# A hybrid decoder layer in float32: linear attention's state formed once per 128 tokens instead of twice, with ten warm-up matmuls, more buffers for the memory's weights, and norms begun three steps later

## The chip, the core and the metric

The kernel runs on one core of one Trainium2 chip. The metric is the device time of one execution in microseconds (us), as the median of several runs. The core's engines are called by short names: PE is TensorE's matmuls, PEld its weight loads, DVE is VectorE, ACT is ScalarE, POOL is GpSimd and SP is SyncE, which here only issues transfers (DMAs).

## What is computed

One decoder layer over 256 tokens of width 2048, in float32. The change touches branch A, the gated linear attention (4 heads, keys of 128, values of 256). With `b` the running sum of the log decay inside a chunk, the reference works on chunks of 64 tokens:

```python
q_e = qc * jnp.exp(b);  k_e = kc * jnp.exp(-b);  k_d = kc * jnp.exp(b_last - b)
s = jnp.where(causal, einsum('bhncd,bhnsd->bhncs', q_e, k_e), 0.0)
o_intra = einsum('bhncs,bhnsv->bhncv', s, vc)
def step(S, inp):                       # once per chunk
    o = einsum('bhcd,bhdv->bhcv', qe, S)
    S = S * dec[..., :, None] + einsum('bhcd,bhcv->bhdv', kd, vv)
    return S, o
```

Branch B is stick-breaking attention (8 heads of 128, queries and keys normed per head). Branch C is softmax attention into 256 memory tokens (4 heads of 256, queries and keys normed), whose keys and values are `rmsnorm(mem) @ w_mem_kv`. Each branch is projected back to 2048, the three are merged by sigmoid gates, projected by `w_o` and added to x; a SwiGLU block of width 5632 follows. Nearly all of the arithmetic is in these dense products.

## The kernel before

**Dense products.** A weight matrix lies in memory in blocks of 512 columns. One load (`raw`, 1 MB) brings 4 row chunks of 128 by 512. ACT makes a high part `wh` (L148) and DVE the rest `wl` (L149), two chunks at a time, and PE multiplies three times for each 128 tokens: high by high, weights' rest by high, high by rest. So one such split of two chunks feeds 12 matmuls of 512 columns in `gemm` (L221 to L223); in `sgemm`, which does one level of Strassen's scheme on 1024 columns, it feeds 6 or 12 (L262 to L265). In `sgemm`, `put` (L302 to L304) copies a finished product out of or into an accumulator. These 512-column matmuls are called the big matmuls below.

**Buffers.** `loads()` (L172) hands out `raw` tiles from the list `free_raw`: three in `ring1` from the start, more when later pools are opened by `widen`. The splits go into the `w` buffers of the same pools (four in `ring1`). PSUM has four `acc` and four `tmp` banks. `loads`, `parts` and every pool's tile wait for the former user of a buffer; SP issues loads in the order of the program.

**Order.** Everything that is not a big matmul is written as Python generators in a list `background`. `step()` advances the first of them by one `yield`, once after each split in `gemm` and `sgemm` (twice for `fine`), so that small work is woven in between big matmuls; `flush()` runs all that is left. What is written thus is then ordered on each engine by the framework's scheduler, which may bring an instruction forward on its own engine.

**Stages that the change touches**, in order of time: eight matmuls of zeros (L563, L564) while the first data comes; the memory's keys and values (`mk`, `mv`; `w_kv`, L584 to L610) with x being loaded beside them (`load_x`); the memory's queries `mq` (L718 to L720); then `sq`, `sk` and `sv_` by `wide` (`sgemm`), each with the work on the one before it in the background: `normed_T` (L489) squares a projection on ACT (L496), sums and scales it on DVE (L497 to L508) and turns it by PE transposes (L520, helper L441), and the memory's attention runs as `m_scores`, `m_turn`, `m_out`, head after head (L667 to L708). `m_out` copies its result to an `out` tile, of which there are two, and sends it off by a DMA from ACT (`put_out`, L640). In `sgemm`, `p6` (L335) has POOL add one weight tile to another by a DMA of 1 MB (L339). Further on, `gla()` (L818) runs beside the projections of branches C and B (`gemm` L974 and L991): for each of two blocks of 128 tokens (`t`), it makes the decay sums by matmuls with constant triangles (L837, L838, L842), the three scaled q and k, turns two of them (L858), forms the scores (L866), and then in two chunks of 64 tokens (`c`): output from the scores (L881), output from the state (L883), the state's increment (L888), and the state itself on DVE (L890, L893).

Of the kernel before, what the change touches and what calls it, by code (L numbers as in the profile page):

```python
# [59 lines left out]
def constants():  # L60
    i, j = np.arange(P)[:, None], np.arange(P)[None, :]
    same = (i // GC) == (j // GC)
    blocks = [
        i == j,
        i < j,
        (i <= j) & same,
        i > j,
        np.ones((P, P), bool),
        (i <= j) & same,
        (i > j) & same,  # L70
        (i // GC) == np.arange(P // GC)[None, :],
    ]
    scale = [1, 1, 1, 1, 1, 1 / TAU, 1 / TAU, 1 / TAU]
    return np.concatenate([b.astype(np.float32) * np.float32(s) for b, s in zip(blocks, scale)], 1)
# [3 lines left out]
def trunk(ctx: ExitStack, tc: tile.TileContext, a, out):  # L78
# [18 lines left out]
    def narrow(pool):  # L97

        for x in (free_raw, splits):
            x[:] = [y for y in x if y[0] is not pool]  # L100
        pool.release()

    pad = tc.alloc_tile_pool(name="pad", bufs=1, side="right")
# [12 lines left out]
    def tmp():  # L116
        return ps.tile([P, NB], F32, tag="tmp", name="tmp", bufs=4)
# [11 lines left out]
    def flush():  # L129
        while background:  # L130
            step()
# [39 lines left out]

    def loads():  # L172

        slot = pool, bufs = free_raw.pop(0)
        return pool.tile([P, KG, NB], F32, tag="raw", name="raw", bufs=bufs), lambda: free_raw.append(slot)

    def parts():

# [307 lines left out]
        for n in range(0, MIX, NB):  # L486
            evac(dst[:, :, n : n + NB], gemm(xs, w, c0 + n), rstd)

    def normed_T(dst, src, heads, dim, gain, scratch):  # L489


        ss = small.tile([P, 2, heads], F32, name="hn_ss")
        for t in range(2):
            for n in range(0, MIX, NB):
                sq = scratch()
                act.activation(sq[:], src[:, t, n : n + NB], AF.Square)  # L496
                dve.tensor_reduce(  # L497
                    ss[:, t, n // dim : (n + NB) // dim],
                    sq[:].rearrange("p (h d) -> p h d", d=dim),
                    axis=AX.X,  # L500
                    op=ALU.add,
                )
            yield
        y = rsqrt_mean(ss[:].rearrange("p t h -> p (t h)"), dim, 2 * heads)
        for t in range(2):
            v = src[:, t].rearrange("p (h d) -> p h d", h=heads)
            dve.tensor_tensor(
                v, v, y[:, t * heads : (t + 1) * heads].unsqueeze(2).to_broadcast([P, heads, dim]), op=ALU.mult  # L508
            )
            yield  # L510
        yield
        e = dim // P
        for c in range(0, 8, 2 * e):
            for q in range(e):

                p = tmp()
                for i in range(2):
                    ch = c + q + i * e
                    for t in range(2):
                        transpose(p[:, i * T + t * P : i * T + (t + 1) * P], src[:, t, ch * P : (ch + 1) * P])  # L520
                d = dst[:, c + q : c + q + e + 1 : e, :]
                act.activation(d, p[:].rearrange("p (c t) -> p c t", c=2), AF.Copy, scale=gain[:, q : q + 1])
                yield
# [20 lines left out]
    def section(name, tag):  # L544
        return sec.tile([P, 2, MIX], F32, tag=tag, name=name)
# [77 lines left out]
    def ra():  # L623
        return ring("ra", 4)

    def rb():
        return ring("rb", 2)
# [97 lines left out]
    wide(sq, O_SQ)  # L725
    flush()
    skT_sv = main.tile([P, 2, 2, MIX], F32, tag="resid", name="skT_sv")
    skT, sv_ = chunks(skT_sv[:, 0]), skT_sv[:, 1]
    sqT = chunks(section("sqT", "b")[:])
    sk = section("sk", "d")  # L730
    background.append(normed_T(sqT, sq, SH, SD, g_sqs, ra))
    wide(sk, O_SK)
# [77 lines left out]
    def pause(n):  # L810
        for _ in range(n):
            yield
# [5 lines left out]
    def gla():  # L818
        for t in range(2):
# [12 lines left out]
            lh, ll = rc(), rd()  # L832
            split(lh[:], ll[:], ls[:])
            yield from pause(4)
            b, bl, dc = tmp(), tmp(), tmp()
            for dst, w in ((b, tri), (bl, rest)):
                pe.matmul(dst[:], w, lh[:], start=True, stop=False)  # L837
                pe.matmul(dst[:], w, ll[:], start=False, stop=True)  # L838
            for h in range(GH):
                for i, l in enumerate((lh, ll)):  # L840
                    pe.matmul(
                        dc[:, 2 * h : 2 * h + 2], l[:, h * GDK : (h + 1) * GDK], ind, start=i == 0, stop=i == 1  # L842
                    )
            qe, ke, kd = ra(), ra(), ra()
            act.activation(qe[:], b[:], AF.Exp)
            act.activation(ke[:], b[:], AF.Exp, scale=-1.0)
            act.activation(kd[:], bl[:], AF.Exp)
# [4 lines left out]
            dve.tensor_tensor(kd[:], gqk[:, t, 512:], kd[:], op=ALU.mult)  # L852
            yield from pause(3)
            turned = []
            for src in (qe, ke):
# [3 lines left out]
                turned.append(rb()[:].rearrange("p (h t) -> p h t", h=GH))  # L859
                dve.tensor_copy(turned[-1].rearrange("p h t -> p (h t)"), p[:])  # L860
                yield from pause(2)
            qeT, keT = turned
            yield from pause(2)
            p = tmp()
            for h in range(GH):
                pe.matmul(p[:, h * P : (h + 1) * P], keT[:, h], qeT[:, h], start=True, stop=True)  # L866
            sT = ra()[:].rearrange("p (h t) -> p h t", h=GH)
            nc.gpsimd.memset(sT, 0.0)
            dve.copy_predicated(sT, causal4, p[:].rearrange("p (h t) -> p h t", h=GH))
# [3 lines left out]
            o = [tmp(), tmp()]  # L873
            ov = [o[h // 2][:, h % 2 * GDV : (h % 2 + 1) * GDV] for h in range(GH)]
            vh = [gv[:, t, h * GDV : (h + 1) * GDV] for h in range(GH)]
            for c in range(2):
                s = slice(c * GC, (c + 1) * GC)
                for h in range(GH):
                    if c == 0:

                        pe.matmul(ov[h], sT[:, h], vh[h], start=h % 2 == 0, stop=False, skip_group_check=True)  # L881
                    if (t, c) != (0, 0):
                        pe.matmul(ov[h][s], qeT[:, h, s], S[h][:], start=False, stop=c == 1, skip_group_check=True)  # L883
                if (t, c) != (1, 1):
                    d = [tmp(), tmp()]
                    for h in range(GH):
                        dh = d[h // 2][:, h % 2 * GDV : (h % 2 + 1) * GDV]
                        pe.matmul(dh, kd[s, h * GDK : (h + 1) * GDK], vh[h][s], start=True, stop=True)  # L888
                        if (t, c) == (0, 0):
                            dve.tensor_copy(S[h][:], dh)  # L890
                        else:
                            f = dec[:, 2 * h + c : 2 * h + c + 1]
                            dve.scalar_tensor_tensor(S[h][:], S[h][:], f, dh, op0=ALU.mult, op1=ALU.add)  # L893
                    yield from pause(3)
# [289 lines left out]
```

## Time and profile before

| What | Value |
| --- | --- |
| Median of 3 runs (lowest to highest) | 1633.13 us (1632.35 to 1633.36) |
| The profiled execution, its own time | 1632.16 us |
| Its span, first to last instruction | 1630.4 us |
| ACT busy | 1028.4 us (63%) |
| DMA share, first to last slice of 40 | 8 tenths in the first, between 4 and 8 after it, 2 in the last |
| From 0.24 to 5.4 us | start, zeros matmuls, first loads |
| From 5.4 to 103 us | memory's keys and values |
| From 157 to 292 us | `sq`, `sk`, `sv_` (most of them) |
| From 439 to 534 us | `gla()` beside the projections of branches C and B |

How to read the views quoted below: a row of the timeline is start, duration, engine, line, operation, output<-inputs, shape, count, and in brackets the engine's idle time before it and what ended that. A matmul's printed duration is from start to result; matmuls overlap, so what one costs in a stream is the distance from its start to the next start. One matmul of float32 operands that are not yet split is two records. The waits view gives the engine, its line, whom it waited for, the total in us, how often, and the longest. The chain view follows the work that ended last: start, length, what.

### The profile page before, as it was taken

Reading aid. Unit: us, or ns where it says so; the run is one execution under the profiler, and the core shown is the slowest. Engines: PE = TensorE matmul, PEld = TensorE weight load, DVE = VectorE, ACT = ScalarE, POOL = GpSimd, SP = SyncE. Lnnn points to the kernel's source line nnn. Section 1 sums busy time; section 2 is a strip of 40 time slices with the busy share of each in tenths; the row PEclk is TensorE's granted clock in tenths of the full one; section 3 lists DMA queues with packets and bytes.
Section 4 is the critical chain, followed back from the end, with each engine's and each line's share of the span. In section 5 each row is a group of like instructions: output and inputs, shape, how many; then the busy total and the mean of one; then the engine's idle time right before and its main releaser. Section 6 shows DMA issues by size and latency. Waiting matters only on the chain.

```text
span 1630.4 us, 19473 instructions
## 1 busy us (share of the span) xinstructions
PE 1620.5 (99%) x7266; PEld 1325.9 (81%) x7266; DVE 1331.5 (82%) x1526; ACT 1028.4 (63%) x1251; POOL 71.2 (4%) x93
## 2 busy tenths in 40 slices
PE   9999999999999999999999999999999999999999
PEld 6888778888877788888888888888888888888887
DVE  6867788877755788897897798988888989888994
ACT  7765576766744666666565566666666666666662
POOL 0000000000000000000000000000110000110000
PEclk9999999999999999999999999999999999999999
DMA  8795667656654888888657768687897687897682
GB/s 328 281 326 161 216 223 247 201 178 203 210 166 165 283 263 257 265 281 301 185 215 234 257 225 265 207 278 245 255 281 243 208 268 255 264 263 246 203 331 92
DMA packets 65888, 390.33 MB, mean 239 GB/s; under 512 B 7265, under 2 KB 13921, under 8 KB 21633
## 3 DMA queue, kind: packets, MB, share of 16 engines
q1 hardware_dynamic: 51344, 324.36, 53.0%
q0 software_dynamic: 11504, 61.87, 19.7%
q10 hardware_dynamic: 2944, 2.85, 0.5%
q8 instruction: 57, 0.93, 0.2%
q14 instruction: 39, 0.31, 0.1%
HBM read 325.09 MB, written 12.58 MB: 207 GB/s over the span
## 4 chain that ended last, share of the span: by engine, by line
PE 96%; DMA 1%; ACT 1%; DVE 1%; issue 0%; ACTq 0%; DVEq 0%
PE acc L262 19%; PE acc L265 19%; PE acc L264 19%; PE acc L221 6%; PE acc L222 6%; PE acc L223 6%; PE tmp L262 6%; PE tmp L265 6%; PE tmp L264 6%; PE tmp L441 2%; ACT wh L148 1%; DMA raw<-in_w_mem_kv 0%; DMA od_mem<-out 0%; DVE wl L149 0%; PE tmp L888 0%; PE tmp L883 0%
## 5 line engine op out<-in xcount | busy, mean ns | idle before, releaser
L149 DVE TENSOR_TENSOR wl<-raw,wh 128x1024 fp32r<-128x1024 f32 (+1 forms) x752 | 904.2, 1220 | 240.0 <-ACT wh L148 227.1
L148 ACT CAST wh<-raw 128x1024 fp32r<-128x1024 f32 (+1 forms) x752 | 783.0, 1052 | 455.1 <-PE acc L265 239.3
L262 PE MATMUL acc<-wh,xTh 128*128 128x512 f32 x504 | 200.6, 399 | 1.7 <-ACT acc L302 1.5
L265 PE MATMUL acc<-wh,xTl 128*128 128x512 f32 x504 | 196.6, 390 | 0.0
L264 PE MATMUL acc<-wl,xTh 128*128 128x512 f32 x504 | 196.4, 390 | 0.0
L262 PE MATMUL acc<-wh,hh 128*128 128x512 f32 x452 | 178.9, 396 | 0.0
L264 PE MATMUL acc<-wl,hh 128*128 128x512 f32 x452 | 176.2, 390 | 0.0
L265 PE MATMUL acc<-wh,hl 128*128 128x512 f32 x452 | 175.1, 390 | 0.0
L277 DVE TENSOR_TENSOR raw<-raw 128x1024 f32<-128x1024 f32 x122 | 147.9, 1220 | 0.7
L221 PE MATMUL acc<-wh,oh 128*128 128x512 f32 x320 | 127.2, 399 | 0.7 <-ACT oh L151 0.6
L222 PE MATMUL acc<-wl,oh 128*128 128x512 f32 x320 | 126.0, 394 | 0.9 <-DVE wl L149 0.9
L223 PE MATMUL acc<-wh,ol 128*128 128x512 f32 x320 | 125.8, 393 | 0.0
L262 PEld LDWEIGHTS acc<-wh,xTh 128*128 128x128 f32 x504 | 94.6, 188 | 24.0 <-ACT acc L302 4.8
L265 PEld LDWEIGHTS acc<-wh,xTl 128*128 128x128 f32 x504 | 94.6, 188 | 20.1
L264 PEld LDWEIGHTS acc<-wl,xTh 128*128 128x128 f32 x504 | 94.7, 188 | 18.8
L262 PE MATMUL tmp<-wh,sh 128*128 128x512 f32 x270 | 106.5, 394 | 0.0
L265 PE MATMUL tmp<-wh,sl 128*128 128x512 f32 x270 | 105.4, 391 | 0.0
L264 PE MATMUL tmp<-wl,sh 128*128 128x512 f32 x270 | 105.3, 390 | 0.0
L262 PEld LDWEIGHTS acc<-wh,hh 128*128 128x128 f32 x452 | 84.9, 188 | 18.7 <-ACT acc L302 1.0
L265 PEld LDWEIGHTS acc<-wh,hl 128*128 128x128 f32 x452 | 84.9, 188 | 17.8
L264 PEld LDWEIGHTS acc<-wl,hh 128*128 128x128 f32 x452 | 85.0, 188 | 16.8
L221 PEld LDWEIGHTS acc<-wh,oh 128*128 128x128 f32 x320 | 60.6, 190 | 17.1 <-issue 3.2
(311 smaller groups left out, 2368.4 us busy)
## 6 DMA issues: line engine op xcount, KB each, us to landing
raw<-in_w_gate_up SPq DMA_DIRECT2D x88, 1024.0 KB, 6.1
raw<-in_w_in SPq DMA_DIRECT2D x56, 1024.0 KB, 5.1
raw<-in_w_gate SPq DMA_DIRECT2D x48, 1024.0 KB, 7.0
raw<-raw POOLq DMA_DIRECT2D x45, 1024.0 KB, 8.0
raw<-in_w_down SPq DMA_DIRECT2D x44, 1024.0 KB, 7.3
raw<-in_w_o SPq DMA_DIRECT2D x16, 1024.0 KB, 5.8
raw<-in_w_mem_kv SPq DMA_DIRECT2D x15, 1024.0 KB, 6.0
raw<-in_w_br_mem SPq DMA_DIRECT2D x8, 1024.0 KB, 5.1
```

What stands on the lines that cost most here:

```text
L148: act.copy(hi, src)
L149: dve.tensor_tensor(lo, src, hi.bitcast(F32), op=ALU.subtract)
L221: pe.matmul(o[t][:], xh[:, s], wh[:, j], start=k == 0, stop=False)
L222: pe.matmul(o[t][:], xh[:, s], wl[:, j], start=False, stop=False)
L223: pe.matmul(o[t][:], xl[:, s], wh[:, j], start=False, stop=k == nk - 1)
L262: pe.matmul(dst[:], xh, wh, start=id(dst) not in begun, stop=False, skip_group_check=True)
L264: pe.matmul(dst[:], xh, wl, start=False, stop=False, skip_group_check=True)
L265: pe.matmul(dst[:], xl, wh, start=False, stop=last, skip_group_check=True)
L277: dve.tensor_tensor(x, x, y, op=ALU.add)
L441: pe.transpose(dst, src, ident)
```

## The change

Five edits:

1. `gla()` forms the state once, after the first 128 tokens. The decay sums run over 128 tokens instead of 64 (constants). Queries of the second 64 tokens exist in two forms: `q2`, scaled from their own chunk's middle sum as before the transpose, and the second half of `qT`, multiplied by the first chunk's decay, so that they can be used against the first chunk's keys and against the state. Scores take two groups of matmuls (`p` over 128 queries, `p2` over the second 64). For `t == 1` no state is formed and no sum `rest` is needed. The state's copies move from DVE to ACT, and the copies of turned queries too.
2. Ten zeros matmuls instead of eight.
3. While the memory's weights are loaded, three `raw` tiles more: two in the place of the Strassen forms (`sh`, `sl`), one in that of section `d`. They are given up before these are used.
4. `normed_T` gets `wait`, a number of yields before it does anything: 3 for `mq`, `sq` and `sk`.
5. The `flush()` between `sq` and `sk` goes; the norm of `sq` is queued before `sk` starts, and its tile is allocated inside the generator.

```diff
@@ constants
-        (i <= j) & same,
+        i <= j,
...
-        (i > j) & same,
+        i > j,
@@ trunk
-        free_raw.extend([(pool, raw)] * raw)
+        free_raw.extend([(pool, raw, "raw")] * raw)
+    def give_up(pool):
+        for x in (free_raw, splits):
+            x[:] = [y for y in x if y[0] is not pool]
@@ loads
-        slot = pool, bufs = free_raw.pop(0)
-        return pool.tile([P, KG, NB], F32, tag="raw", name="raw", bufs=bufs), lambda: free_raw.append(slot)
+        slot = pool, bufs, tag = free_raw.pop(0)
+        return pool.tile([P, KG, NB], F32, tag=tag, name="raw", bufs=bufs), lambda: free_raw.append(slot)
@@ normed_T
-    def normed_T(dst, src, heads, dim, gain, scratch):
+    def normed_T(dst, src, heads, dim, gain, scratch, wait=0):
+        for _ in range(wait):
+            yield
@@ start
+    free_raw.extend([(fpool, 1, "sh"), (fpool, 1, "sl"), (sec, 1, "d")])
-    for _ in range(8):
+    for _ in range(10):
         pe.matmul(idle[:], zeros[:, :P], zeros[:], start=True, stop=True)
...
     xs = [x() for x in xs]
+    give_up(fpool)
+    give_up(sec)
     mempool.release()
@@ queries and keys
-    background.append(normed_T(mqT, mq, MH, MD, g_mq, ra))
+    background.append(normed_T(mqT, mq, MH, MD, g_mq, ra, 3))
     background.append(pipelined((m_scores, m_turn, m_out), MH, 1))
     sq = section("sq", "a")
     wide(sq, O_SQ)
-    flush()
...
-    background.append(normed_T(sqT, sq, SH, SD, g_sqs, ra))
+    def q_T():
+        sqT.append(chunks(section("sqT", "b")[:]))
+        yield from normed_T(sqT[0], sq, SH, SD, g_sqs, ra, 3)
+    background.append(q_T())
...
     wide(sk, O_SK)
     flush()
-    background.append(normed_T(skT, sk, SH, SD, g_sk, ra))
+    background.append(normed_T(skT, sk, SH, SD, g_sk, ra, 3))
@@ gla
-            b, bl, dc = tmp(), tmp(), tmp()
-            for dst, w in ((b, tri), (bl, rest)):
+            sums = [(tri, tmp())] + ([(rest, tmp())] if t == 0 else [])
+            dc = tmp()
+            for w, dst in sums:
...
+            qT = ra()[:].rearrange("p (h t) -> p h t", h=GH)
+            q2 = rb()[:, :T].rearrange("p (h t) -> p h t", h=GH)
+            act.copy(qT[:, :, :GC], p[:, :, :GC])
+            dve.tensor_tensor(qT[:, :, GC:], p[:, :, GC:], first_64, op=ALU.mult)
+            act.copy(q2, p[:, :, GC:])
...
+                pe.matmul(p[:, h * P : (h + 1) * P], keT[:, h], qT[:, h], start=True, stop=True)
+                pe.matmul(p2[:, h * GC : (h + 1) * GC], keT[:, h], q2[:, h], start=True, stop=True)
...
-            for c in range(2):
-                s = slice(c * GC, (c + 1) * GC)
-                for h in range(GH):
-                    if c == 0:
-                        pe.matmul(ov[h], sT[:, h], vh[h], start=h % 2 == 0, stop=False, skip_group_check=True)
-                    if (t, c) != (0, 0):
-                        pe.matmul(ov[h][s], qeT[:, h, s], S[h][:], start=False, stop=c == 1, skip_group_check=True)
-                if (t, c) != (1, 1):
...
-                        pe.matmul(dh, kd[s, h * GDK : (h + 1) * GDK], vh[h][s], start=True, stop=True)
...
-                            dve.scalar_tensor_tensor(S[h][:], S[h][:], f, dh, op0=ALU.mult, op1=ALU.add)
+            for h in range(GH):
+                pe.matmul(ov[h], sT[:, h], vh[h], start=h % 2 == 0, stop=t == 0, skip_group_check=True)
+                if t == 1:
+                    pe.matmul(ov[h], qT[:, h], S[h][:], start=False, stop=True, skip_group_check=True)
+            if t == 0:
+                d = pairs_of([tmp(), tmp()])
+                for h in range(GH):
+                    pe.matmul(d[h], kd[:, h * GDK : (h + 1) * GDK], vh[h], start=True, stop=True)
+                    act.copy(S[h][:], d[h])
+            yield from pause(3)
```

Three places where the order of instructions moves.

**PE, linear attention, first 128 tokens.** Rows are in the order in which PE takes them. `gv,ra` are values with scores (L881) or values with scaled keys (L888), `S` is the state. The rows before the change, without most of the big matmuls between the groups:

```order
L881 MATMUL tmp<-gv,ra 128x256 x4
L888 MATMUL tmp<-gv,ra 128x256 x2
L221 MATMUL acc<-wh,oh 128x512
L888 MATMUL tmp<-gv,ra 128x256 x2
```

```order
L883 MATMUL tmp<-S_3679,rb 64x256
L883 MATMUL tmp<-S_3680,rb 64x256
L883 MATMUL tmp<-S_3681,rb 64x256
L883 MATMUL tmp<-S_3682,rb 64x256
L888 MATMUL tmp<-gv,ra 128x256 x2
```

The same place of the changed kernel (L917 is the former L881, L923 the former L888):

```order
L917 MATMUL tmp<-gv,ra 128x256 x4
L923 MATMUL tmp<-gv,ra 128x256 x2
L224 MATMUL acc<-wh,oh 128x512
L923 MATMUL tmp<-gv,ra 128x256 x2
L225 MATMUL acc<-wl,oh 128x512
```

The first group stays, in a form that covers 128 tokens; the second group (and two more matmuls L888 just behind it) is gone, and the next row of `gla()` is the start of the second 128 tokens, 60 rows further on.

**SP, the first loads of the memory's weights.** DMAHW and DVE are the semaphores that a load waits for: a former transfer on the same semaphore, and DVE's last reading of the buffer. Before:

```order
L209 DMA raw<-in_w_mem_kv 128x1024
L455 DMA xraw<-in_memT 128x2x256
L455 DMA xraw<-in_memT 128x2x256 [waits DMAHW0_49]
L209 DMA raw<-in_w_mem_kv 128x2048 [waits DMAHW1_49,DVE_49]
L455 DMA xraw<-in_memT 128x2x256 [waits DMAHW2_49]
```

After:

```order
L212 DMA raw<-in_w_mem_kv 128x1024
L458 DMA xraw<-in_memT 128x2x256
L458 DMA xraw<-in_memT 128x2x256 [waits DMAHW0_49]
L212 DMA raw<-in_w_mem_kv 128x2048 [waits DMAHW1_49]
L458 DMA xraw<-in_memT 128x2x256 [waits DMAHW2_49]
```

The order is the same; the first load of 1 MB no longer waits for DVE.

**ACT, from the end of `sq` into `sk`.** `ra<-sq` are the norm's squares, `acc<-tmp` is the copy of `put` for `sk`, `out<-tmp` and the DMA behind it are a head of the memory's attention leaving. Before:

```order
L644 COPY out<-tmp 128x256 x2
L645 DMA od_mem<-out 128x256 x2
L714 ACTIVATE sq<-acc,r_x 128x512
L496 ACTIVATE ra<-sq 128x512 x2
L148 CAST wh<-raw 128x1024
L714 ACTIVATE sq<-two,r_x 128x512
L148 CAST wh<-raw 128x1024
L496 ACTIVATE ra<-sq 128x512
L302 COPY acc<-tmp 128x512
```

After:

```order
L653 COPY out<-tmp 128x256 x2
L654 DMA od_mem<-out 128x256 x2
L703 COPY rb<-tmp 128x512
L501 ACTIVATE ra<-sq 128x512 x2
L305 COPY acc<-tmp 128x512
L151 CAST wh<-raw 128x1024
L653 COPY out<-tmp 128x256 x2
L654 DMA od_mem<-out 128x256 x2
L501 ACTIVATE ra<-sq 128x512 x2
```

Before, the last head's output and three of the four squares stand ahead of `put`'s copy; after, two squares do, and the last head's output stands behind it. On PE, the four heads' `m_out` come after 679, 708, 732 and 744 big matmuls of the program before, and after 708, 732, 756 and 768 now.

More of the change, by code (lines that the diff above doesn't have):

```diff
@@ L725, in trunk @@
     wide(sq, O_SQ)
+    sqT = []
+    def q_T():
+        sqT.append(chunks(section("sqT", "b")[:]))
+        yield from normed_T(sqT[0], sq, SH, SD, g_sqs, ra, 3)
+    background.append(q_T())
+    sk = section("sk", "d")
+    wide(sk, O_SK)
     flush()
+    sqT = sqT[0]
     skT_sv = main.tile([P, 2, 2, MIX], F32, tag="resid", name="skT_sv")
     skT, sv_ = chunks(skT_sv[:, 0]), skT_sv[:, 1]
-    sqT = chunks(section("sqT", "b")[:])
-    sk = section("sk", "d")
-    background.append(normed_T(sqT, sq, SH, SD, g_sqs, ra))
-    wide(sk, O_SK)
-    flush()
-    background.append(normed_T(skT, sk, SH, SD, g_sk, ra))
+    background.append(normed_T(skT, sk, SH, SD, g_sk, ra, 3))
     wide(sv_, O_SV)
@@ L843, in gla @@
                     )
-            qe, ke, kd = ra(), ra(), ra()
+            b = sums[0][1]
+            qe, ke = ra(), ra()
             act.activation(qe[:], b[:], AF.Exp)
             act.activation(ke[:], b[:], AF.Exp, scale=-1.0)
-            act.activation(kd[:], bl[:], AF.Exp)
             dec = small.tile([P, 2 * GH], F32, name="g_dec")
@@ L851, in gla, with turned @@
             dve.tensor_tensor(ke[:], gqk[:, t, 512:], ke[:], op=ALU.mult)
-            dve.tensor_tensor(kd[:], gqk[:, t, 512:], kd[:], op=ALU.mult)
+            if t == 0:
+                kd = ra()
+                act.activation(kd[:], sums[1][1][:], AF.Exp)
+                dve.tensor_tensor(kd[:], gqk[:, t, 512:], kd[:], op=ALU.mult)
             yield from pause(3)
-            turned = []
-            for src in (qe, ke):
+            def turned(src):
                 p = tmp()
@@ L858, in gla @@
                     transpose(p[:, h * P : (h + 1) * P], src[:, h * GDK : (h + 1) * GDK])
[L859 to L862, printed above, removed]
-            yield from pause(2)
-            p = tmp()
+                return p[:].rearrange("p (h t) -> p h t", h=GH)
+            p = turned(qe)
+            qT = ra()[:].rearrange("p (h t) -> p h t", h=GH)
+            q2 = rb()[:, :T].rearrange("p (h t) -> p h t", h=GH)
+            act.copy(qT[:, :, :GC], p[:, :, :GC])
+            first_64 = dec[:].rearrange("p (h c) -> p h c", h=GH)[:, :, :1].to_broadcast([P, GH, GC])
+            dve.tensor_tensor(qT[:, :, GC:], p[:, :, GC:], first_64, op=ALU.mult)
+            act.copy(q2, p[:, :, GC:])
+            yield from pause(2)
+            p = turned(ke)
+            keT = rb()[:].rearrange("p (h t) -> p h t", h=GH)
+            dve.tensor_copy(keT, p)
+            yield from pause(3)
+            p, p2 = tmp(), tmp()
             for h in range(GH):
-                pe.matmul(p[:, h * P : (h + 1) * P], keT[:, h], qeT[:, h], start=True, stop=True)
+                pe.matmul(p[:, h * P : (h + 1) * P], keT[:, h], qT[:, h], start=True, stop=True)
+            for h in range(GH):
+                pe.matmul(p2[:, h * GC : (h + 1) * GC], keT[:, h], q2[:, h], start=True, stop=True)
             sT = ra()[:].rearrange("p (h t) -> p h t", h=GH)
             nc.gpsimd.memset(sT, 0.0)
-            dve.copy_predicated(sT, causal4, p[:].rearrange("p (h t) -> p h t", h=GH))
+            dve.copy_predicated(sT[:GC], causal4[:GC], p[:].rearrange("p (h t) -> p h t", h=GH)[:GC])
+            dve.copy_predicated(
+                sT[GC:, :, GC:], causal4[GC:, :, GC:], p2[:, :T].rearrange("p (h t) -> p h t", h=GH)[GC:]
+            )
             yield from pause(3)
@@ L872, in gla, with pairs_of @@
             ss = small.tile([P, GH], F32, name="g_ss")
-            o = [tmp(), tmp()]
-            ov = [o[h // 2][:, h % 2 * GDV : (h % 2 + 1) * GDV] for h in range(GH)]
             vh = [gv[:, t, h * GDV : (h + 1) * GDV] for h in range(GH)]
-            for c in range(2):
-                s = slice(c * GC, (c + 1) * GC)
-                for h in range(GH):
-                    if c == 0:
-                        pe.matmul(ov[h], sT[:, h], vh[h], start=h % 2 == 0, stop=False, skip_group_check=True)
-                    if (t, c) != (0, 0):
-                        pe.matmul(ov[h][s], qeT[:, h, s], S[h][:], start=False, stop=c == 1, skip_group_check=True)
-                if (t, c) != (1, 1):
-                    d = [tmp(), tmp()]
-                    for h in range(GH):
-                        dh = d[h // 2][:, h % 2 * GDV : (h % 2 + 1) * GDV]
-                        pe.matmul(dh, kd[s, h * GDK : (h + 1) * GDK], vh[h][s], start=True, stop=True)
[L889 to L892, printed above, removed]
-                            dve.scalar_tensor_tensor(S[h][:], S[h][:], f, dh, op0=ALU.mult, op1=ALU.add)
-                    yield from pause(3)
+            def pairs_of(into):
+                return [into[h // 2][:, h % 2 * GDV : (h % 2 + 1) * GDV] for h in range(GH)]
+            ov = pairs_of([tmp(), tmp()])
+            for h in range(GH):
+                pe.matmul(ov[h], sT[:, h], vh[h], start=h % 2 == 0, stop=t == 0, skip_group_check=True)
+                if t == 1:
+                    pe.matmul(ov[h], qT[:, h], S[h][:], start=False, stop=True, skip_group_check=True)
+            if t == 0:
+                d = pairs_of([tmp(), tmp()])
+                for h in range(GH):
+                    pe.matmul(d[h], kd[:, h * GDK : (h + 1) * GDK], vh[h], start=True, stop=True)
+                    act.copy(S[h][:], d[h])
+            yield from pause(3)
             for h in range(GH):
```

3 lines of the change are left out of this document (2 added, 1 removed).

## Prediction

> **What bounds the kernel now.** I read the page's busy times first, then the chain of work that ended last, then PE's waits, and last the timeline at the places that the change touches.
>
> ```profile
> PE 1620.5 (99%) x7266; PEld 1325.9 (81%) x7266; DVE 1331.5 (82%) x1526; ACT 1028.4 (63%) x1251; POOL 71.2 (4%) x93
> PE 96%; DMA 1%; ACT 1%; DVE 1%; issue 0%; ACTq 0%; DVEq 0%
> PE acc L262 <- ACT acc L302: 1.5, 2, 1.3
> ```
>
> The first row is busy time by engine, the second the chain's share by engine, the last is the entry at the head of PE's waits (total, times, longest). PE is busy 99% of the span and carries 96% of the chain; its waits are single events of 1 us or so. So the time is PE's time: an edit is worth the matmuls that it takes from PE plus the few waits that it removes, and nothing that it does to the other engines counts until PE waits for it.
>
> **Part 1: the state once per 128 tokens.** The rows are PE's, start and then duration. In them 470.34 is the first row of a group of small matmuls, and 475.04 the first big matmul that is back in the ordinary step; likewise for the other pairs.
>
> ```profile
> 469.88 0.39 PE L222 MATMUL acc<-wl,oh 128*128 128x512 f32 x1
> 470.11 0.39 PE L223 MATMUL acc<-wh,ol 128*128 128x512 f32 x1
> 470.34 1.89 PE L881 MATMUL tmp<-gv,ra 128*128 128x256 f32 x8
> 475.04 0.40 PE L223 MATMUL acc<-wh,ol 128*128 128x512 f32 x1
> ...
> 478.78 1.94 PE L883 MATMUL tmp<-S,rb 128*64 128x256 f32 x8
> 484.00 0.39 PE L222 MATMUL acc<-wl,oh 128*128 128x512 f32 x1
> ...
> 519.54 0.59 PE L881 MATMUL tmp<-gv,ra 128*128 128x256 f32 x2
> 527.76 0.40 PE L221 MATMUL acc<-wh,oh 128*128 128x512 f32 x1
> 531.26 1.94 PE L883 MATMUL tmp<-S,rb 128*64 128x256 f32 x8
> 533.47 0.40 PE L222 MATMUL acc<-wl,oh 128*128 128x512 f32 x1
> ```
>
> A big matmul costs the step from 469.88 to 470.11, 0.23 us. The four stretches last 4.70, 5.22, 8.22 and 2.21 us. Of the big matmuls woven into them (2, 4, 3 and 1) I take off 0.23 each, which leaves 4.24 + 4.30 + 7.53 + 1.98 = 18.05 us for the 64 records of outputs and increments (L881, L883, L888). The change issues 32 such records, all over 128 rows. What one costs in a group is in the chain:
>
> ```profile
> 182.83 1.73 PE tmp L701 x8
> 448.87 0.25 PE L841 MATMUL tmp<-cr,rc 128*128 128x2 f32 x1
> 448.98 0.25 PE L841 MATMUL tmp<-cr,rd 128*128 128x2 f32 x1
> L866 PE MATMUL tmp<-rb 128*128 128x128 f32 x16 | 2.1, 274 | 0.0
> ```
>
> Eight records of the same form (128x256) took 1.73 us, 0.216 each. So 32 take 6.9 us, and with 0.1 us for leaving each of three groups (474.71 to 475.04 in the trace was 0.33 and not 0.23) 7.2. That saves 10.85 us. Two matmuls with the triangle go as well, at 0.23 each: 0.5 saved. Added is `p2`: eight products of 128x64, sixteen records. No row has that form. Those of 128x2 follow at 0.11 us, those of 128x128 (the last row: 2.1 us busy in 16) at 0.13; half of the latter, 0.07, is the lower end. I take the 0.11 of the smaller form: 1.8 us, with 1.0 and 2.1 as ends. **Term 1 is -10.85 - 0.5 + 1.8 = -9.6 us**, from -9.0 to -10.6.
>
> What could hide in it is a wait. In the changed order 18 big matmuls (4.1 us) stand between the turning of the keys and the scores, and as many between the scores and the output, where 24 and 36 stood. In the 4.1 us DVE has one copy to make and at worst one weights' rest ahead of it. The state's copies move to ACT, which is 63% busy, and the state is used only by the second block, some 10 us later. So I take no wait. If the cover fails it should cost what PE's wait for an ACT copy cost at 198 us, 1.1 us, in one or two places. That the decay sums run over 128 tokens changes constants alone. On POOL one transfer of the gates now stands ahead of two stores; POOL is 4% busy and PE waits for nothing of it here, so it is taken as nothing, and any delay of it falls under the 1.1 us above.
>
> **Part 2: norms begun later, no flush between `sq` and `sk`.** The rows are PE's timeline, and then pieces of the chain and POOL's transfer.
>
> ```profile
> 157.24 0.39 PE L262 MATMUL acc<-wh,xTh 128*128 128x512 f32 x1
> 157.86 0.41 PE L441 MATMUL tmp<-cst,mq 128*128 128x128 f32 x2 [0.23 <-DVE mq L507]
> ...
> 196.78 0.40 PE L265 MATMUL acc<-wh,xTl 128*128 128x512 f32 x1
> 198.28 1.99 PE L701 MATMUL tmp<-rb,mv_mqT 128*128 128x256 f32 x8 [1.11 <-ACT rb L694]
> ...
> 207.19 0.39 PE L265 MATMUL acc<-wh,xTl 128*128 128x512 f32 x1
> 208.91 0.50 PE L262 MATMUL acc<-wh,xTh 128*128 128x512 f32 x1 [1.33 <-ACT acc L302]
> ...
> 363.87 0.45 PE L262 MATMUL acc<-wh,xTh 128*128 128x512 f32 x1
> 364.48 0.50 PE L262 MATMUL acc<-wh,xTh 128*128 128x512 f32 x1 [0.17 <-DVE acc L304]
> ```
>
> ```profile
> 193.76 0.86 POOL L339 DMA_DIRECT2D raw<-raw  x1 [36.01 <-DVE ra L685]
> 194.92 7.21 DMA od_mem<-out
> 202.21 0.66 ACT out L644 x2
> 207.84 0.53 ACT ra L496
> 208.37 0.49 ACT acc L302
> ```
>
> Against the step of 0.23, PE lost 0.39 us at 157, 1.27 at 197 and 1.49 at 207: 3.15 together. The second block tells why. POOL issued its 1 MB transfer at 193.76, the head's output left behind it at 194.92 and took 7.21 us; with two `out` tiles the next copy could start only at 202.21, and ACT, which works in order, ran late from there: a square (207.84) stood ahead of `put`'s copy (208.37), on which PE's next matmul waited. In the changed order each of the last three heads comes 24 big matmuls later (5.4 us), when POOL's transfer should have landed; two squares instead of three stand ahead of `put`'s copy, and the last head's output stands behind it. A put without such a queue still costs about 0.38 us (0.61 from 363.87 to 364.48, less 0.23), so of 1.49 some 1.1 goes; 1.27 and 0.39 go, and a few tenths at the later norms. **Term 2 is -3.0 us**, between 0 (the waits move with the heads) and -3.5.
>
> **Part 3: the start.** Rows of PE's timeline, of the chain, and of a window of 2 us (busy us by engine, then the granted clock, the DMA share, GB/s).
>
> ```profile
> 8.96 0.63 PE L223 MATMUL acc<-wh,ol 128*128 128x512 f32 x1
> 9.39 0.56 PE L221 MATMUL acc<-wh,oh 128*128 128x512 f32 x1
> 9.79 0.39 PE L222 MATMUL acc<-wl,oh 128*128 128x512 f32 x1
> 11.22 0.51 PE L222 MATMUL acc<-wl,oh 128*128 128x512 f32 x1 [0.35 <-DVE wl L149]
> ...
> 5.56 7.27 DMA raw<-in_w_mem_kv
> 12.86 1.06 ACT wh L148
> 13.94 1.24 DVE wl L149
> 15.22 0.50 PE acc L222
> 7.00:9.00 2.00, 1.00 1.00 348
> ```
>
> Until 9.39 a big matmul steps by 0.43 us, from 9.79 by 0.23. Two more zeros matmuls, at 0.43 each, run in PE's gap before 5.38 and end at about 5.46: +0.1 at most. But PE waits for data at 11.22, and at 15.22 for the load issued at 5.56, which landed at 12.83 and passed ACT and DVE. That load will no longer wait for a buffer and can be issued some 0.8 us earlier, behind loads that keep all DMA engines busy (share 1.00), so it should land hardly earlier. **Term 3 is -0.1 us**, from +0.1 to -0.8. What the other loads of the memory's weights gain by the three buffers is hidden by the matmuls of splits already made: after 15.22 the timeline has no wait of PE for a split until 146 us.
>
> The Trainium skill has a rule that speaks otherwise. Its page "TensorE: Matmul & The Clock Gate", section "🔬 Part 1: The HAM clock gate (the "warmup" mystery)", says that the clock doubles after one busy window of about 3.4 us, that the window runs freely, and that a stream with a hole may miss it. The trace agrees with the doubling (0.43 to 0.23 at 9.39) but can't show where a window begins. By that rule an unbroken warm-up might end the slow stretch one window sooner; by the wait at 15.22 it would change nothing.
>
> **Sum.** -9.6 - 3.0 - 0.1 = -12.7 us. The profiled execution took 1632.16; less 12.7 is 1619.5. The median of the runs is 0.97 above that execution, so I forecast **1620.5 us**.
>
> **Rivals.**
>
> *B, only the matmuls pay.* The norm's waits move with the heads: `m_out` again waits for the softmax of its head, or the next `put` stands behind other work of ACT. For it: each of these chains of ACT, DVE and DMA still exists and PE is 99% busy. Against it: they get 5.4 us more. Then 1633.1 - 9.7 = **1623.5 us**.
>
> *C, the start pays too.* The clock doubles before real work begins, and the loads keep up: the ten matmuls that begin from 5.38 to 9.39 save 0.2 us each, 2.0 us, so **1618.5 us**. Against it are the waits at 11.22 and 15.22: data, not the clock, sets the start. This is the rule named above.
>
> *D, slower, by the last piece of x.* In the built order the split of the last piece of x on DVE stands one weight split ahead of the first product of `w_in`, where five stood before, and its load stands on SP behind two loads of 1 MB. In the view of SP's waits the worst wait for a buffer was:
>
> ```profile
> SPq L209 <- DVE wl L149: 171.2, 39, 14.2
> ```
>
> A split feeds 12 big matmuls, 2.7 us. Three or four splits of slack are 8 to 11 us, say 9.5. One slot wait of 14.2 us and a landing of 7.3 (the load of 5.56) would leave PE idle for 12 us, 1632.5 in all, no loss yet. It decides from 16 us idle on, when the piece comes some 25 us late: two such slot waits one behind the other, 28.4 + 7.3 - 9.5 = 26 us idle, would give **1646.7 us**. The cover is the loads' lead before that place; three more buffers make it longer.
>
> *E, no effect.* The buffers are never taken and the scheduler orders the norms as before, with terms 2 and 3 at zero: this is B's time. For no effect at all, 32 matmuls would have to cost PE nothing, and the four stretches exclude that.
>
> **How the numbers follow.** My forecast has a chance of 0.65, B 0.2, C 0.1, and 0.05 is left for a wait in `gla()` of 2 us and more or for D. The range begins below C, with term 1 at its better end (1618.5 - 1.0, and half a us for run to run), at 1617; it ends above B with a failed cover in two places (1623.5 + 2.2), at 1626. About 0.2% (3.3 us) is what a measurement of this kernel can tell from no change: faster than that means under 1629.9. All cases but D lie there: 0.94 faster, 0.04 within, 0.02 slower.
>
> **What would show it.** In the changed profile: PE's small matmuls of `gla()` in groups of eight at 0.216 each, with no idle time ahead of the output; no idle time of over 0.5 us on PE between 157 and 215 us; a step of 0.43 us until 9 to 10 us and a wait near 15 us as before. It is wrong if PE waits anew where the last piece of x is needed, at about 103 us, if `p2` costs more than 2.1 us, or if a wait of 1 us stands again in front of L710 (the former L701) or behind `put`.

## The result, and the profile after

| Kernel | Median of its runs, us | Runs of before beside it, us | Ratio to before, 95% interval |
| --- | --- | --- | --- |
| changed | 1618.15 (1617.37 to 1621.23, 5 runs) | 1632.35 | 0.9914, 0.99 to 0.9929 |

The changed kernel is 14.2 us faster; forecast were 1620.5 us and 12.6 us less (from the 1633.13 of the kernel before that was known then), within 1617 to 1626. The profiled execution took 1618.15 us, with a span of 1616.4.

The first fence has rows of the changed kernel's page (busy time by engine; the chain's share by engine). Line numbers are the changed kernel's: L224 to L226 are the former L221 to L223, L265 to L268 the former L262 to L265, L710 the former L701, L305 the former L302.

```profile
PE 1607.8 (99%) x7250; PEld 1323.1 (82%) x7250; DVE 1326.8 (82%) x1515; ACT 1031.3 (64%) x1258; POOL 71.2 (4%) x93
PE 98%; DMA 1%; ACT 0%; DVE 0%; issue 0%; SPq 0%; DVEq 0%
```

PE is still 99% busy; its busy time fell by 12.7 us and the rest of the 14.0 us of span is idle time that went. PE's waits in the changed kernel:

```profile
PE acc L224 <- ACT wh L151: 1.2, 2, 1.0
PE tmp L571 <- DVE zeros L568: 1.2, 1, 1.2
PE acc L225 <- DVE wl L152: 1.1, 2, 0.5
PE acc L224 <- ACT oh L154: 0.9, 1, 0.9
PE acc L265 <- DVE acc L307: 0.2, 1, 0.2
```

All but the last lie in the first 16 us. The waits of `m_out` on `rb` and of a big matmul on `put`'s ACT copy, at 198 and 208 us before, are gone (the row with 0.2 is the one that stood at 364 us before), and `gla()` has none.

Where the time went is read by taking the n-th big matmul of both programs (each has 6678, and their sequence is the same) and subtracting its start before from its start after:

| Big matmul (counted from 0), its start before | changed | gla_alone | norms_alone | start_alone |
| --- | --- | --- | --- | --- |
| 30, 16.25 us | +0.11 | -0.29 | -0.39 | -0.76 |
| 640, 156.79 us | +0.14 | -0.29 | +0.34 | -0.76 |
| 1000, 262.10 us | -3.72 | +3.42 | -3.04 | +0.71 |
| 1700, 446.67 us | -3.80 | +3.41 | -3.05 | +0.72 |
| 2100, 566.41 us | -14.08 | -6.90 | -3.04 | +0.86 |
| last, 1626.12 us | -14.00 | -6.99 | -2.65 | +0.95 |

In the changed kernel the start gives +0.1, the stretch of the norms (640th to 1000th) -3.86, `gla()` (1700th to 2100th) -10.28, and nothing else moves by more than 0.1. (`norms_alone` loses 0.7 us between the 30th and the 640th, at a wait of 0.45 us for DVE's split at 37.3 us that before does not have.)

### The profile page after: what moved, and what is told of

It reads as the page before. It is cut to its first block, busy times and chain, and to the rows that moved or that the text cites. A ratio compares the mean times of both kernels' runs of the same rounds, so it can differ in the third digit from the quotient of the medians.

```text
span 1616.4 us, 19439 instructions
## 1 busy us (share of the span) xinstructions
PE 1607.8 (99%) x7250; PEld 1323.1 (82%) x7250; DVE 1326.8 (82%) x1515; ACT 1031.3 (64%) x1258; POOL 71.2 (4%) x93
## 4 chain that ended last, share of the span: by engine, by line
PE 98%; DMA 1%; ACT 0%; DVE 0%; issue 0%; SPq 0%; DVEq 0%
PE acc L265 19%; PE acc L268 19%; PE acc L267 19%; PE tmp L265 6%; PE tmp L267 6%; PE tmp L268 6%; PE acc L225 6%; PE acc L224 6%; PE acc L226 6%; PE tmp L444 2%; DMA raw<-in_w_mem_kv 0%; PE tmp L682 0%; PE tmp L710 0%; DMA xraw<-in_memT 0%; PE tmp L917 0%; ACT wh L151 0%
## 5 line engine op out<-in xcount | busy, mean ns | idle before, releaser
L265 PE MATMUL acc<-wh,xTh 128*128 128x512 f32 x504 | 200.5, 398 | 0.2 <-DVE acc L307 0.2
L268 PE MATMUL acc<-wh,xTl 128*128 128x512 f32 x504 | 196.2, 390 | 0.0
L265 PE MATMUL acc<-wh,hh 128*128 128x512 f32 x452 | 178.9, 396 | 0.0
L268 PE MATMUL acc<-wh,hl 128*128 128x512 f32 x452 | 175.1, 390 | 0.0
L224 PE MATMUL acc<-wh,oh 128*128 128x512 f32 x320 | 126.4, 396 | 2.1 <-ACT wh L151 1.2
L226 PE MATMUL acc<-wh,ol 128*128 128x512 f32 x320 | 124.9, 390 | 0.0
L265 PEld LDWEIGHTS acc<-wh,xTh 128*128 128x128 f32 x504 | 94.6, 188 | 21.9 <-ACT acc L305 2.7
L268 PEld LDWEIGHTS acc<-wh,xTl 128*128 128x128 f32 x504 | 94.6, 188 | 20.1
L265 PE MATMUL tmp<-wh,sh 128*128 128x512 f32 x270 | 106.2, 393 | 0.0
L268 PE MATMUL tmp<-wh,sl 128*128 128x512 f32 x270 | 105.3, 390 | 0.0
L265 PEld LDWEIGHTS acc<-wh,hh 128*128 128x128 f32 x452 | 84.8, 188 | 18.7 <-ACT acc L305 1.0
L268 PEld LDWEIGHTS acc<-wh,hl 128*128 128x128 f32 x452 | 84.8, 188 | 18.0
L224 PEld LDWEIGHTS acc<-wh,oh 128*128 128x128 f32 x320 | 59.9, 188 | 16.8 <-ACT wh L151 2.1
```

The costliest lines, as they stand in the source:

```text
L224: pe.matmul(o[t][:], xh[:, s], wh[:, j], start=k == 0, stop=False)
L226: pe.matmul(o[t][:], xl[:, s], wh[:, j], start=False, stop=k == nk - 1)
L265: pe.matmul(dst[:], xh, wh, start=id(dst) not in begun, stop=False, skip_group_check=True)
L268: pe.matmul(dst[:], xl, wh, start=False, stop=last, skip_group_check=True)
```

## The experiments

Each edit is a difference against the kernel that the expectation names. All ran beside the kernel before on one chip for each group of runs.

**First group: each part alone, and the first load.** `gla_alone`, `norms_alone` and `start_alone` are the kernel before with the lines of the diff above that belong to edit 1, to edits 4 and 5, and to edits 2 and 3.

> The kernel before with edit 1 alone (the state once per 128 tokens). The matmuls' theory: the 10.3 us that the distance between the two programs' big matmuls grows by from 417 to 566 us is this edit's own, so the time is 10.3 us below before, and PE's three waits at 157, 198 and 208 us stay (0.39, 1.27 and 1.49 us). Rival: part of the 10.3 us came from the norms' edits, which shifted the loads; then the gain is under 9 us.

> The kernel before with edits 4 and 5 alone (norms three yields later, no flush). My theory: 3.9 us below before, as the distance between the big matmuls grows by 3.94 us from 16 to 413 us in the changed kernel, with no wait of over 0.5 us on PE between 157 and 215 us. Rival: the three raw buffers of edit 3 had a share in it, by earlier loads; then the gain is under 3 us.

> The kernel before with edits 2 and 3 alone (ten zeros matmuls, three more buffers at the start). Data's theory: 0 to 0.3 us from before, with a wait of PE that ends near 15.3 us, whether the step of 0.43 us ends at 4 or at 10 us. The clock's theory: where the clock doubles before 6 us, 1.5 to 2 us below before.

The fourth changes one line of the changed kernel:

```diff
-    o = gemm(mems, w_kv, 0, first=(1, 1, 2))
+    o = gemm(mems, w_kv, 0, first=(1, 1, 2, 2, 2))
```

> The changed kernel with the first product's two loads of 1 MB as four of 512 KB. Data's theory: PE waits for the first 1 MB load, which lands at 12.94 us although only half of it is wanted first; in halves that first half lands about 1.3 us earlier, the wait that ends at 15.3 ends at about 14, and the time is 1.0 to 1.5 us below the changed kernel's, about 15.4 below before. If something else than this landing sets the start, no change against the changed kernel (14.2 below before).

| Kernel | Median, us | Before beside it, us | Ratio, 95% interval |
| --- | --- | --- | --- |
| gla_alone | 1623.01 (1622.22 to 1625.16) | 1634.52 (1631.29 to 1637.05) | 0.993, 0.9917 to 0.9942 |
| norms_alone | 1629.37 (1628.14 to 1630.91) | the same | 0.9968, 0.9955 to 0.998 |
| start_alone | 1632.89 (1631.97 to 1635.96) | the same | 0.9992, 0.9983 to 1.0001 |
| halves | 1616.97 (1616.73 to 1618.02) | the same | 0.9893, 0.9879 to 0.9906 |

The runs of the kernel before beside these spread from 1631.29 to 1637.05 us, six of fifteen above 1636. By the medians the three parts are 11.5, 5.2 and 1.6 us faster, which is together more than the whole change; so the shares are read from the profiles, one execution of each. `gla_alone` gains 10.31 us between the 1700th and the 2100th big matmul, as the changed kernel does (10.28): the edit's gain is its own, as expected. `norms_alone` gains 3.38 us between the 640th and the 1000th, where 3.9 was expected, with no wait over 0.5 us there. `start_alone` is 0.76 us ahead after the start and loses 1.5 at the norms, which it doesn't touch; its 1.6 us by the medians lie between its two theories, with an interval that reaches no change.

The three show something else. The stall at the end of `sq` isn't of one size, and `gla_alone`'s expectation that the waits of before would stay as they were did not hold. ACT's timeline at that place, in the kernel before and then in `gla_alone`, whose order there is the same:

```profile
194.92 2.68 ACTq L645 DMA_DIRECT2D od_mem<-out  x2
197.65 0.58 ACT L694 COPY rb<-tmp 128x512 f32<-128x512 f32 x1 [2.48 <-PE acc L265]
...
202.21 0.65 ACT L644 COPY out<-tmp 128x256 f32<-128x256 f32 x2 [1.47 <-DMA od_mem<-out]
```

```profile
194.64 1.53 ACTq L645 DMA_DIRECT2D od_mem<-out  x2
196.22 0.59 ACT L694 COPY rb<-tmp 128x512 f32<-128x512 f32 x1 [1.33 <-PE tmp L441]
...
202.87 0.65 ACT L644 COPY out<-tmp 128x256 f32<-128x256 f32 x2 [3.56 <-DMA od_mem<-out]
```

And PE's timeline there in `gla_alone`, then a window behind the wait (us busy by engine with instructions; granted clock, DMA share, GB/s):

```profile
205.74 0.39 PE L265 MATMUL acc<-wh,xTl 128*128 128x512 f32 x1
209.96 0.80 PE L262 MATMUL acc<-wh,xTh 128*128 128x512 f32 x1 [3.84 <-ACT acc L302]
210.56 0.63 PE L264 MATMUL acc<-wl,xTh 128*128 128x512 f32 x1
210.99 0.63 PE L265 MATMUL acc<-wh,xTl 128*128 128x512 f32 x1
```

```profile
211.00:214.00 3.00, 3.00 (x9) 2.33 (x8) 2.23 (x6) 0.00 (x0) 0.00 (x0) 0.50 0.20 30
```

Here ACT stood for 3.56 us for an `out` tile, and PE for 3.84 us, where before it was 1.47 and 1.33. Behind that wait the clock was granted at half (0.50) and a big matmul stepped by 0.43 us, 12 of them from 209.96 to 215.25. The longer wait is 2.5 us and the slow steps 2.4; PE's wait of 1.1 us at 198 us is not there (ACT issued its DMAs in 1.53 us and not 2.68). Together that is 3.8 us, and it is why `gla_alone`'s profile falls 3.7 us behind before between the 640th and the 1000th big matmul, and why that execution was the longest of its five. `start_alone`'s profile has the same wait at 3.58 us, without the halved clock.

**Second group: the norms taken apart, and no warm-up.** In `waits_alone` only the argument `wait` is added. In `more_outs` only `put_out` differs:

```diff
+        both = rc() if o is od_mem else None
         for i in range(src.shape[1] // T):
-            v = att.tile([P, T], F32, name="out", tag="out", bufs=2)
+            if both is None:
+                v = att.tile([P, T], F32, name="out", tag="out", bufs=2)[:]
+            else:
+                v = both[:, i * T : (i + 1) * T].bitcast(F32)
...
```

> The kernel before with edit 4 alone: the norms wait three yields, the flush between sq and sk stays. My theory: the wait alone moves the first three heads off POOL's transfer, but the flush now runs the last head's turning and its output with no big matmul between them, so PE waits there for ACT's copy about as long as it waited at 198 us before (1.3 us, up to 2.5 with a transpose's result): 0.5 to 2.5 us less gain than both edits together (3.4 us by the run of both), that is 1 to 3 us below before. Rival: the flush cost nothing, and the time is that of both edits.

> The kernel before with four places for a head's output instead of two (halves of the tiles rc, which nothing else uses at that time), all else in its place. If the wait of put at 208 us (1.5 us in the first profile, 3.7 to 4.0 in two runs with the same order there) is ACT waiting for an out tile whose DMA lies behind POOL's transfer, it falls to under 0.8 us, with the copy of the next head's output at about 199 us and not at 202: 0.7 to 3.3 us below before. If ACT is late there for the squares and casts alone, the wait stays at 1.5 us or more.

`no_zeros` is the changed kernel with this line, and `best` joins the edits of `halves` and `more_outs` to the changed kernel:

```diff
-    for _ in range(10):
+    for _ in range(0):
```

> The changed kernel without any warm-up matmul. Data's theory: PE starts cold at about 5.4 us, does its first 12 big matmuls by about 10.5 and the next 12 at worst by 15.7, when the load of 1 MB has been split anyway: 0 to 1.5 us above the changed kernel. The clock's theory (rival C of the prediction): the slow stretch is one or two windows longer, 12 to 16 matmuls at 0.2 us: 2.4 to 3.2 us above.

> The changed kernel with the first two 1 MB loads in halves and with four places for a head's output. If both theories hold: no wait of PE at 15.3 us, none over 0.3 us between 157 and 215 us, 1.0 to 1.7 us below the changed kernel. If the first stretch of 3.4 us with idle time in it sets the clock back, as it did in the profile of the halves (0.43 us a step from 11.8 to 14.8), the halves gain nothing and the time is within 0.5 us of the changed kernel.

| Kernel | Median, us | Before beside it, us | Ratio, 95% interval |
| --- | --- | --- | --- |
| waits_alone | 1631.57 (1630.04 to 1633.61) | 1632.78 (1631.97 to 1637.13) | 0.999, 0.9982 to 0.9999 |
| more_outs | 1631.25 (1630.04 to 1632.04) | the same | 0.9988, 0.9979 to 0.9997 |
| no_zeros | 1618.18 (1618.16 to 1619.54) | the same | 0.9911, 0.9897 to 0.9924 |
| best | 1616.64 (1616.35 to 1618.74) | the same | 0.9902, 0.9888 to 0.9915 |

`waits_alone` and `more_outs` are 1.2 and 1.5 us faster than before by the medians, both within what was expected. PE's timeline in `waits_alone` has one long wait in this stretch:

```profile
200.72 1.99 PE L703 MATMUL tmp<-rb,mv_mqT 128*128 128x256 f32 x8 [2.17 <-ACT rb L696]
```

It is the last head, whose turning and output the flush runs without a big matmul between them. Between the 640th and the 1000th big matmul it gains 1.43 us, against 3.38 for both edits: the flush's removal is worth 2.0 us, once the heads are late. In the kernel before, the last head is done on PE after 744 big matmuls, and `waits_alone`'s flush runs it after 756. So with the old waits that flush had no head left to run, and its removal alone should have been worth little; that was not run.

PE's timeline in `more_outs`, at `m_out` of the last head and at the matmul behind `put`, and then ACT's:

```profile
197.99 1.99 PE L705 MATMUL tmp<-rb,mv_mqT 128*128 128x256 f32 x8 [1.24 <-ACT rb L698]
...
206.86 0.39 PE L265 MATMUL acc<-wh,xTl 128*128 128x512 f32 x1
207.08 0.46 PE L262 MATMUL acc<-wh,xTh 128*128 128x512 f32 x1
```

```profile
194.49 2.81 ACTq L649 DMA_DIRECT2D od_mem<-rc  x2
197.35 0.58 ACT L698 COPY rb<-tmp 128x512 f32<-128x512 f32 x1 [2.61 <-PE acc L265]
...
200.35 0.64 ACT L648 COPY rc<-tmp 128x256 f32<-128x256 f32 x2
```

The wait behind `put` is gone: with a free place the last head's copy starts at 200.35 and not at 202.21, and all behind it on ACT is earlier, though squares and casts stand ahead of `put` as before. The wait at 198 stays (1.24 us): it is ACT's issue of two DMAs, which took 2.81 us (2.68 before), and not the landing. The other profiles agree: with an issue of 1.87 us (`start_alone`) PE waited there 0.3 us, with 1.53 (`gla_alone`) not at all. So the two waits at 198 and 208 us, which the prediction put down to one cause, have two.

`no_zeros` takes as long as the changed kernel. Its PE timeline at the start, and then the chain:

```profile
5.94 0.79 PE L224 MATMUL acc<-wh,oh 128*128 128x512 f32 x1 [5.94 <-ACT oh L154]
...
10.80 0.63 PE L226 MATMUL acc<-wh,ol 128*128 128x512 f32 x1
11.23 0.91 PE L224 MATMUL acc<-wh,oh 128*128 128x512 f32 x2
11.97 0.39 PE L225 MATMUL acc<-wl,oh 128*128 128x512 f32 x1
...
15.28 0.50 PE L225 MATMUL acc<-wl,oh 128*128 128x512 f32 x1 [0.42 <-DVE wl L152]
```

```profile
5.18 7.71 DMA raw<-in_w_mem_kv
12.92 1.06 ACT wh L151
14.00 1.24 DVE wl L152
```

All of the first 12 real matmuls are slow, and PE still comes to 14.2 us in time to wait for the load that landed at 12.9. At the 30th big matmul it stands at +0.08 to before, the changed kernel at +0.11. Data sets the start; the warm-up is worth nothing here. `best` kept both expectations in its profile: no wait at 15.3 us, none over 0.2 between 157 and 215.

**Third group: the changed kernel beside two that start finer.** `quarters` has `first=(1, 1, 1, 1, 2, 2)` in place of `best`'s `(1, 1, 2, 2, 2)`.

> The changed kernel once more, beside the two below on one chip: a wait of PE that ends at 15.3 us or a little earlier, whenever the step of 0.43 us ends, and 1618 us give or take 0.5.

> The changed kernel with the first two 1 MB loads in halves and four places for a head's output, once more: 1.5 us below the changed kernel where PE isn't slowed again after its waits at 9 to 11 us, within 0.5 us of it where it is.

> As best_again, with the 512 KB load of chunks 2 and 3 as two of 256 KB as well. Data's theory: PE's waits that end at 9.5 and 10.7 us (1.7 us over the ordinary step) fall by the half load's 0.65 us or more: 0.5 to 1.2 us below best_again. If ACT and DVE, which then split one chunk at a time, set the start: no change or up to 0.5 us slower.

| Kernel | Median, us | Before beside it, us | Ratio, 95% interval |
| --- | --- | --- | --- |
| after_again | 1617.58 (1617.49 to 1619.08) | 1633.64 (1632.05 to 1635.22) | 0.9906, 0.9892 to 0.992 |
| best_again | 1616.67 (1616.21 to 1618.79) | the same | 0.99, 0.9886 to 0.9914 |
| quarters | 1618.31 (1617.54 to 1618.75) | the same | 0.9907, 0.9893 to 0.9921 |

`best_again` is 0.9 us below the changed kernel by its median, but its longest run is above the changed kernel's shortest. The profile is of that run (1618.79 us). Its PE timeline and three windows:

```profile
8.21 0.39 PE L226 MATMUL acc<-wh,ol 128*128 128x512 f32 x1
10.75 0.73 PE L224 MATMUL acc<-wh,oh 128*128 128x512 f32 x2 [2.15 <-ACT wh L151]
12.01 0.80 PE L225 MATMUL acc<-wl,oh 128*128 128x512 f32 x1 [0.53 <-DVE wl L152]
12.61 0.63 PE L226 MATMUL acc<-wh,ol 128*128 128x512 f32 x1
```

```profile
8.00:10.75 2.75, 0.60 (x3) 0.18 (x1) 0.90 (x3) 2.00 (x4) 0.00 (x0) 1.00 1.01 352
12.00:15.30 3.30, 3.29 (x8) 2.62 (x9) 3.19 (x6) 3.04 (x6) 0.00 (x0) 0.50 1.07 421
15.50:17.00 1.50, 1.50 (x8) 1.23 (x7) 1.50 (x4) 0.91 (x3) 0.00 (x0) 1.00 1.12 386
```

PE waited for data from 8.4 to 12 us, with two matmuls between, and then ran at half the clock until 15.3. In the profile of `best`, the same kernel (1616.35 us), the load in question landed 1.3 us earlier and the clock was not halved; at the 30th big matmul `best_again` stands 2.8 us behind it, 1.3 by the later landing and 1.5 by the clock. The profile of `halves` (1618.02 us, the longest of its four) has the halved clock too: waits of 0.98 and 0.52 us with two matmuls between, then 0.43 us a step from 11.8 to 14.8, and at the 30th big matmul nothing is left of the gain (+0.23).

The medians of `halves`, `best` and `best_again` lie 0.9 to 1.5 us below the changed kernel's, under 0.1%. Nine of their twelve runs took 1616.2 to 1617.1 us, less than the shortest of the changed kernel's ten (1617.37); the other three took 1618.0 to 1618.8, and the two of these that were profiled had the halved clock. So halved first loads look worth about 1 us where the clock holds; the changed kernel ran beside them in one group only, and how often the clock falls is not shown. `quarters` missed its expectation: it came 1.6 us above `best_again`, and gains nothing over the changed kernel. At the 30th big matmul it is 1.57 us ahead of before, but 0.5 is lost at 19.6 us around a wait for DVE and 0.8 at 675 us to a wait for ACT, in the one execution profiled.

## Why the prediction was right, and where its sizes were off

The mechanism of the two large terms held: fewer matmuls in `gla()` and shorter waits at the norms. The time came 2.35 us under the forecast, of which 1.3 are the terms below; the other 1.0 is what was added for the runs' median, while the changed kernel's profiled execution is its median. That the measured 1618.15 lies nearer to rival C's 1618.5 than to the forecast is luck: the gain that C named did not come (term 3).

**Term 1, the state: -9.6 forecast, -10.3 measured.** The rows of the changed kernel's PE timeline that answer to the prediction's four stretches, and the scores with `p2` (L899):

```profile
457.02 1.00 PE L899 MATMUL tmp<-rb 128*128 128x64 f32 x8
457.83 0.48 PE L224 MATMUL acc<-wh,oh 128*128 128x512 f32 x1
...
462.05 1.89 PE L917 MATMUL tmp<-gv,ra 128*128 128x256 f32 x8
464.45 0.59 PE L224 MATMUL acc<-wh,oh 128*128 128x512 f32 x1
465.61 0.58 PE L225 MATMUL acc<-wl,oh 128*128 128x512 f32 x1
466.03 0.39 PE L226 MATMUL acc<-wh,ol 128*128 128x512 f32 x1
...
505.06 0.59 PE L917 MATMUL tmp<-gv,ra 128*128 128x256 f32 x2
508.32 0.58 PE L224 MATMUL acc<-wh,oh 128*128 128x512 f32 x1
508.74 0.40 PE L225 MATMUL acc<-wl,oh 128*128 128x512 f32 x1
```

Two stretches are left: 3.98 less two big matmuls, and 3.68 less one, 3.52 + 3.45 = 6.97 us where 7.2 was forecast, against 18.05. `p2` follows at 0.10 us a record (0.81 for eight), so 1.6 and not 1.8. With the two triangle matmuls that is -11.1 - 0.5 + 1.6 = -10.0. The other 0.3 is what is left of small differences both ways in rows that both kernels have: by the steps from start to start, the triangles' two were 0.6, the scores of 128x128 cost 0.16 more, and the big matmuls behind other groups some 0.4 less. No wait came: the cover of 18 big matmuls held.

**Term 2, the norms: -3.0 forecast, -3.9 measured, and its account of the waits was in part wrong.** The 0.38 us that was kept for a put wasn't paid at that place: the matmul behind it came without a wait. The later norms gave the tenths that were named. Two things were not as told. The wait at 198 us was put down to the late landing and was ACT's issue (`more_outs`). And the heads were to come "when POOL's transfer should have landed", which they do not. The changed kernel's timelines of POOL and of ACT:

```profile
189.45 0.85 POOL L342 DMA_DIRECT2D raw<-raw  x1 [31.56 <-DVE ra L694]
```

```profile
189.70 0.65 ACT L653 COPY out<-tmp 128x256 f32<-128x256 f32 x2
190.10 0.81 ACTq L654 DMA_DIRECT2D od_mem<-out  x2
...
199.53 0.64 ACT L653 COPY out<-tmp 128x256 f32<-128x256 f32 x2
```

A head's output leaves right behind POOL's transfer still, and its two DMAs take 9.3 and 9.1 us to land by the trace: POOL's transfer lands at 199.2 us, they at 199.4 and 199.6. Only it is the second head now, and the next one comes 24 big matmuls behind it where the last came 12 behind the third. Its copy found the tiles free by about a tenth of a us. In `norms_alone` it did not: ACT waited 0.72 us there, and PE 0.24. So the edit moved the collision to where there is more time, and didn't remove it. And the size of the gain is that of a stall that was 1.3 us in one execution and 3.8 in another: beside executions of the kernel before with the long stall the change is worth more, with no merit of its own.

**Term 3, the start: -0.1 forecast, +0.1 measured.** The step of 0.43 us that was to stand until 9 to 10 us was not there. Rival C's first premise came true, a clock that doubles before real work, and its gain did not. PE's timeline of the changed kernel:

```profile
1.19 3.72 PE L571 MATMUL tmp<-zeros 128*128 128x512 bf16 x10 [1.19 <-DVE zeros L568]
5.82 0.50 PE L224 MATMUL acc<-wh,oh 128*128 128x512 f32 x1 [0.91 <-ACT oh L154]
...
10.05 0.73 PE L224 MATMUL acc<-wh,oh 128*128 128x512 f32 x2 [1.04 <-ACT wh L151]
11.31 0.50 PE L225 MATMUL acc<-wl,oh 128*128 128x512 f32 x1 [0.53 <-DVE wl L152]
```

Ten zeros took 3.72 us and not ten times 0.43: the clock doubled among them, and no real matmul stepped by 0.43 (from the fourth on it was 0.23). PE was 1.4 us ahead of before by 8.4 us, and spent it all in waiting for the loads; at 15.32 it stood where it had stood at 15.22. The load behind that wait was issued at 5.17 and not at 5.56, 0.4 us earlier where 0.8 was forecast, and landed no earlier (12.94 and 12.84). `no_zeros` shows the same from the other side. The +0.1 is no cost of the edits: at the 30th big matmul the five profiled programs with the old start stand between -0.87 and 0 to before, and the changed kernel, `after_again` and `start_alone` between -0.76 and +0.11. The Trainium skill, "TensorE: Matmul & The Clock Gate", section "🔬 Part 1: The HAM clock gate (the "warmup" mystery)", has the window run freely; by that the moment of doubling is partly chance, and the runs agree: with ten zeros it came at about 4.1 us in one execution and at about 5.4 in another. The spread is wider still: with ten zeros it came at about 7 in `quarters`, and with eight it had come by the first real matmul (5.6) in `waits_alone` and `more_outs`, and came between 9.4 and 10.7 in before, `norms_alone` and `gla_alone`. So one profile of each can't tell what two more zeros did to the clock.

**B, D and E** did not come. The sum was 1.3 us short, 0.7 of it in term 1 and 0.9 in term 2, less 0.2 in term 3.

## What to carry to other kernels

Where one engine is 99% busy, count its instructions and price them by the step from start to start, from rows of the same form: that gave the large term to within a tenth of its size. A wait for a buffer is worth what the transfer behind it takes in that execution: look for what its DMA queues behind, and give the next user more distance, or more places. Before warming a clock, look for the first wait for data that a faster engine would run into.

## What the runs showed of the hardware

- A stretch in which PE waits can halve its clock for the next 3 to 5 us: after idle times of 3.84 us (`gla_alone`), of 2.15 and 0.53 us with two matmuls between (`best_again`), and of 0.98 and 0.52 (`halves`), the granted clock was 0.50 and the step 0.43 us. After 3.58 us in one piece (`start_alone`), and after 1.04 and 0.53 with two matmuls between (the changed kernel), it was not. So length alone doesn't decide it, and a short stall may cost twice.
- The issue of two DMAs of 128 KB from ACT took 2.68 us before, 2.81 in `more_outs`, 1.87 in `start_alone`, 1.53 in `gla_alone`, and 0.81 in the changed kernel, in the same part of the program and each time behind POOL's transfer. Why is open; ACT does nothing else meanwhile.
- A DMA of 128 KB from ACT, which took 1.9 to 2.5 us in four issues from 199.9 us on in the changed kernel, took 9.1 to 9.3 at 190 us behind one of 1 MB on POOL's queue, though it was issued on another. In each of the 13 profiles the two DMAs issued behind that transfer landed after it, the first within 0.3 us; what holds them is not shown.
